# First gates of a two-block kernel: x in four transfers, squares summed pair by pair, rstd spread from its own column; HGRN2 scores of both directions in one call

## The chip, the cores and the metric

The kernel runs on one core of a Trainium2 chip. The metric is the device time of one execution in microseconds; lower is better. The time before is 875.5 us, the median of three runs (874.65 to 876.54).

## The reference

Two transformer-like blocks on 256 latent tokens and 256 context tokens of width 1024, all in 32-bit floats. The change touches the opening of the first block and the core of its HGRN2 mixer.

```python
m_l = (sc_lat @ w_ada + b_ada); m_c = sc_ctx @ w_ada + b_ada   # shift, scale, gate ...
hl = modulate(rmsnorm(lat, norm_g[0]), sh1, sc1)               # x*rstd*g*(1+scale)+shift
hc = modulate(rmsnorm(cx, norm_g[0]), csh1, csc1)
...
q, zf_fwd, zf_bwd, v, g = split(h @ w_in, 5)                   # per direction d:
f = lb[d] + (1 - lb[d]) * sigmoid(zf); logf = log(f); k = 1 - f
...
b = cumsum(logf)                                               # in chunks of 64
qe = q * exp(b - b_ref); ke = k * exp(b_ref - b)
scores = where(tril, qe @ ke.T, 0)
o = scores @ v + (q * exp(b)) @ s_start                        # both directions are added
```

After that come the mixer's readout, a convolutional feed-forward layer, and the second block with retention, windowed attention and a squared-ReLU layer; the change leaves them alone.

## The kernel before

Activations stand feature by token: xT is eight tiles (k = 0 to 7) of 128 features by 512 tokens, the context's 256 and the latents' 256. Every weight tile is split into a high part `hi` (ACT, L155) and a low part `lo` (DVE, L156), every activation likewise into hTh and hTl, and a dense product is three matmuls, hi·hi, hi·lo and lo·hi (`mm3`, L352 to L354). PSUM has two sets of four banks, "x" and "m".

All loads stand in one list `halves` in the order of use. `pump` issues them on SP's queue into eight buffers `raw` of 512 KB, as these come free, and emits the splits up to a limit; `use` takes the next chunk of the list. ACT, DVE and TensorE each work in program order, so the order of the code is the order on the engine.

First gates (L438 to L532). SP's queue brings xT in eight transfers, the identity, and then by turns the ada pieces (`ada1`, 1 MB each in two halves, used unsplit) and the f0 weights (256 KB each). 36 filler matmuls (`WARM`) on ones keep TensorE busy meanwhile. x is squared and added up over k, the array sums over features (L473), `rstd_of` makes a scale and a power on GpSimd (L319), DVE puts the four columns on a diagonal `dg` (L477), and one 512-column matmul with ones spreads it over the partitions (L487). `x_r` multiplies a tile of x by it. `ada_mm(k)` (L403) makes shift and scale of the features of tile k from the ada piece, four column groups at a time; `feat(k)` (L412, L413) turns them into columns A and B; `feat_hi` and `feat_lo` make h = x·r·A + B and its two parts. The loop over k then lays f0's four output tiles (forget gates of head pair 0, both directions): one output tile, the feature chain of k + 1 with its splits, three more, then `ada_mm(k + 2)`; the order is written out in `plan`.

HGRN2 (from L618). Head pairs p = 0 to 3. Per pair and direction `gates` makes scaled keys and queries on ACT and DVE, then `hg_side` gives small steps for TensorE: T_ (transposes of keys kc, copied by ACT to kcT at L627), SC_(hh, d) (scores of one head and direction), S_ (state, L633), O_ (output), OT_ (transpose). The steps of pairs 0 to 2 are queued in `side` and `tick` runs the next one at fixed places of the following pair's dense products; two score steps fall on one place. Those of the last pair stand in `slots` (L867 on), at four places in each of the four g products.

SC_ (L638) fills one PSUM bank: eight matmuls whose output takes 32 partitions (L647, L649), one 128-wide (L652), two 64-wide (L658). DVE then copies the kept entries under the mask (L664), ACT copies the rest (L666, L671), and after the second direction DVE adds both into scm.

## Time and profile before

| | |
|---|---|
| time, median of 3 | 875.5 us |
| the profiled execution: time | 873.8 us |
| its span, first to last instruction | 872.0 us |
| TensorE busy | 856.8 us (98%) |
| VectorE busy | 599.5 us (69%) |
| ScalarE busy | 497.8 us (57%) |
| granted TensorE clock, mean | 0.997 |

The span is shorter than the time by 1.8 us, which lie around it. A TensorE that counts as busy need not be at its peak: matmuls overlap, and at a low granted clock they last longer. So the share says where to look, and the timeline of a stretch says what is won there. All times below are microseconds from the start of the span.

### The profile page before, as it was taken

Reading aid. Unit: us, or ns where it says so; the run is one execution under the profiler, and the core shown is the slowest. Engines: PE = TensorE matmul, PEld = TensorE weight load, DVE = VectorE, ACT = ScalarE, POOL = GpSimd, SP = SyncE. Lnnn points to the kernel's source line nnn. Section 1 sums busy time; section 2 is a strip of 40 time slices with the busy share of each in tenths; the row PEclk is TensorE's granted clock in tenths of the full one; section 3 lists DMA queues with packets and bytes.
Section 4 is the critical chain, followed back from the end, with each engine's and each line's share of the span. In section 5 each row is a group of like instructions: output and inputs, shape, how many; then the busy total and the mean of one; then the engine's idle time right before and its main releaser. Section 6 shows DMA issues by size and latency. Waiting matters only on the chain.

```text
span 872.0 us, 15429 instructions
## 1 busy us (share of the span) xinstructions
PE 856.8 (98%) x6216; PEld 778.4 (89%) x6216; DVE 599.5 (69%) x935; ACT 497.8 (57%) x807; POOL 16.3 (2%) x27
## 2 busy tenths in 40 slices
PE   8999999999999999999999999999999999999997
PEld 7688898989978999999998799999999899999995
DVE  5577969776888688977768646765485687555532
ACT  4587474855856666555555646666553675444421
POOL 0000000000000000000000000000000100000000
PEclk9999999999999999999999999999999999999999
DMA  9893653825437368776753574545696097566401
GB/s 355 277 337 109 184 180 125 287 73 170 144 123 240 122 214 272 265 240 203 259 179 85 157 218 119 147 144 165 196 309 201 6 317 247 184 190 190 148 1 49
DMA packets 116360, 161.99 MB, mean 186 GB/s; under 512 B 13888, under 2 KB 95808, under 8 KB 116288
## 3 DMA queue, kind: packets, MB, share of 16 engines
q1 hardware_dynamic: 113984, 155.80, 55.4%
q10 hardware_dynamic: 2304, 5.20, 1.8%
q8 instruction: 49, 0.80, 0.4%
q14 instruction: 23, 0.19, 0.1%
HBM read 159.93 MB, written 1.05 MB: 185 GB/s over the span
## 4 chain that ended last, share of the span: by engine, by line
PE 89%; DVE 5%; ACT 3%; DMA 1%; issue 1%; POOL 0%; SPq 0%; POOLq 0%; DVEq 0%; ACTq 0%
PE m L352 17%; PE m L353 17%; PE m L354 17%; PE x L352 8%; PE x L353 8%; PE x L354 8%; PE x L691 1%; DVE lo L156 1%; PE m L342 1%; PE x L342 1%; PE m L343 1%; PE m L338 1%; PE x L343 1%; PE x L338 1%; DMA raw<-in_f0w_dram 1%
## 5 line engine op out<-in xcount | busy, mean ns | idle before, releaser
L156 DVE TENSOR_TENSOR lo<-raw,hi 128x1024 fp32r<-128x1024 f32 (+1 forms) x248 | 291.1, 1204 | 128.4 <-ACT hi L155 124.5
L155 ACT ACTIVATE hi<-raw 128x1024 fp32r<-128x1024 f32 (+1 forms) x248 | 249.6, 1039 | 115.9 <-PE x L353 47.7
L352 PE MATMUL m<-hT,hi 128*128 128x256 f32 (+1 forms) x560 | 178.2, 318 | 1.4 <-ACT hT L428 1.4
L353 PE MATMUL m<-hT,hi 128*128 128x256 f32 (+1 forms) x560 | 170.5, 304 | 0.5 <-DVE hT L435 0.5
L354 PE MATMUL m<-hT,lo 128*128 128x256 f32 (+1 forms) x560 | 170.8, 305 | 0.1
L352 PE MATMUL x<-hT,hi 128*128 128x256 f32 x592 | 166.5, 281 | 0.0
L353 PE MATMUL x<-hT,hi 128*128 128x256 f32 x592 | 165.9, 280 | 0.0
L354 PE MATMUL x<-hT,lo 128*128 128x256 f32 x592 | 165.9, 280 | 0.0
L352 PEld LDWEIGHTS m<-hT,hi 128*128 128x128 f32 x560 | 105.6, 189 | 12.2 <-issue 5.1
L354 PEld LDWEIGHTS x<-hT,lo 128*128 128x128 f32 x592 | 113.0, 191 | 0.0
L352 PEld LDWEIGHTS x<-hT,hi 128*128 128x128 f32 x592 | 111.4, 188 | 1.0 <-ACT hi L155 0.2
L353 PEld LDWEIGHTS x<-hT,hi 128*128 128x128 f32 x592 | 111.1, 188 | 1.0 <-issue 0.2
L353 PEld LDWEIGHTS m<-hT,hi 128*128 128x128 f32 x560 | 105.7, 189 | 5.9 <-DVE hT L435 1.1
L354 PEld LDWEIGHTS m<-hT,lo 128*128 128x128 f32 x560 | 105.4, 188 | 5.8 <-DVE lo L156 0.3
L352 PE MATMUL m<-hi,ah 128*128 128x512 f32 x248 | 96.7, 390 | 0.0
L354 PE MATMUL m<-hi,al 128*128 128x512 f32 x248 | 96.6, 390 | 0.0
L353 PE MATMUL m<-lo,ah 128*128 128x512 f32 x248 | 96.6, 389 | 0.0
L354 PEld LDWEIGHTS m<-hi,al 128*128 128x128 f32 x248 | 46.6, 188 | 9.8 <-DVE al L1149 0.2
L353 PEld LDWEIGHTS m<-lo,ah 128*128 128x128 f32 x248 | 46.6, 188 | 8.8
L352 PEld LDWEIGHTS m<-hi,ah 128*128 128x128 f32 x248 | 46.5, 188 | 8.7
L582 DVE SCALAR_TENSOR_TENSOR vr<-raw,cs,vr 128x1024 f32<-128x1024 f32 x28 | 35.9, 1281 | 0.4
L352 PE MATMUL m<-hi,hT 128*128 128x256 f32 x128 | 35.8, 280 | 0.0
(302 smaller groups left out, 1250.7 us busy)
## 6 DMA issues: line engine op xcount, KB each, us to landing
raw<-in_ffn_w_up_dram SPq DMA_DIRECT2D x44, 512.0 KB, 5.6
raw<-in_w_in_dram SPq DMA_DIRECT2D x42, 512.0 KB, 4.1
raw<-in_hg_w_in_dram SPq DMA_DIRECT2D x36, 512.0 KB, 5.0
raw<-in_w_ada_dram SPq DMA_DIRECT2D x32, 512.0 KB, 5.0
raw<-in_w_up_dram SPq DMA_DIRECT2D x32, 512.0 KB, 4.7
raw<-in_w_down_dram SPq DMA_DIRECT2D x32, 512.0 KB, 3.7
raw<-in_ffn_w_down_dram SPq DMA_DIRECT2D x22, 512.0 KB, 4.3
raw<-in_ada_dram SPq DMA_DIRECT2D x16, 512.0 KB, 6.2
```

The lines of the kernel that those rows point to most:

```text
L155: s_.activation(h[:, :w], r[:, :w], AF.Copy)
L156: held.append(lambda r=r, h=h, l=l, w=w: v_.tensor_tensor(l[:, :w], r[:, :w], h[:, :w].bitcast(F32), op=OP.subtract))
L338: t_.matmul(o, hTl[:, k, c], w[k][0], start=False, stop=k == KT - 1)
L342: t_.matmul(o, hTh[:, k, c], w[k][0], start=k == 0, stop=False)
L343: t_.matmul(o, hTh[:, k, c], w[k][1], start=False, stop=False)
L352: t_.matmul(o, wh, xh, start=start, stop=False)
L353: t_.matmul(o, wh, xl, start=False, stop=False)
L354: t_.matmul(o, wl, xh, start=False, stop=stop)
L582: v_.scalar_tensor_tensor(acc, w[kk][0], cs[:, k:k + 1], acc, op0=OP.mult, op1=OP.add)
L691: t_.matmul(z[:, b * 128:(b + 1) * 128], l, r, start=i == 0, stop=i == len(terms) - 1)
```

## The change

- xT comes in four transfers of two tiles each (the host lays it out so that a partition's row of a transfer is 4 KB). The ada pieces leave the list of `halves`: they have eight buffers of their own, four pieces deep (`ADA_BUFS`), loaded by `load_ada`; f0's loads are let out one by one behind them (`lim`), and only after the last ada piece the rest of the list.
- 9 fillers in place of 36. The bank of the sums is cleared by a 512-column matmul with zeros; every pair of squared tiles is added and summed by four 128-column matmuls onto it, with one or two fillers behind.
- r is spread by four matmuls that take a column of r, broadcast, against the identity. `ada_mm(0)` and `feat(0)` go ahead of that, `ada_mm(1)` between it and the first f0 product.
- A and r go into one multiplication (`feat_h`), B into the ACT copy for hTh and into the low part. For k = 0 all eight products with hTh go first, the four with hTl last.
- The mask is stored as bytes. The lower bounds are worked out in the loop; ACT loads the table of Exp there and then that of Sigmoid again.
- `SC_(hh)` does both directions: two 128-wide matmuls, then 24 with an output of 32 partitions in turn over the four column groups, then both directions' copies. The last pair's slots put both score steps behind the state steps, and the output steps one place later.

```diff
+ADA_BUFS = 4
-WARM = 36
+WARM = 9
...
-    C["xT"] = add([([(lambda t, k=k: xT[:, k, :], a["xcT"][k]) for k in range(KT)]
+    C["xT"] = add([([(lambda t, k=k: xT[:, k:k + 2, :], a["xcT"][:, k:k + 2, :]) for k in range(0, KT, 2)]
                     + [(lambda t: ident, a["ident"])], 1, 512)], "own")
...
-    def ada_mm(k, w):
+    def load_ada(k):
+        ar[k] = [p0.tile([128, 4, 256], F32, tag="ar", name="ar", bufs=2 * ADA_BUFS) for _ in range(2)]
+        for j in range(2):
+            nc.sync.dma_start(ar[k][j], a["ada1"][k, :, j])
+
+    def load_f0(n=1):
+        at_["lim"] += n
+        pump(0)
+
+    def ada_mm(k):
         rw = bank("x")
         for kk in range(KT):
             g = slice(kk % 4 * 32, kk % 4 * 32 + 32)
-            t_.matmul(rw[g, :256], c2[:, kk, :], w[kk][0], start=kk < 4, stop=kk >= 4)
-        rs[k] = p0.tile([128, 256], F32, tag="rs", name="rs")
+            t_.matmul(rw[g, :256], c2[:, kk, :], ar[k][kk // 4][:, kk % 4, :], start=kk < 4, stop=kk >= 4)
+        rs[k] = p0.tile([128, 256], F32, tag="rs", name="rs", bufs=2)
+        if k + ADA_BUFS < KT:
+            load_ada(k + ADA_BUFS)
+            load_f0(1 if k + ADA_BUFS < KT - 1 else 1 << 20)
         return lambda: s_.activation(rs[k], rw[:, :256], AF.Copy)
-
-    def x_r(k, r_):
-        v_.tensor_mul(xT[:, k, :], xT[:, k, :], r_)
...
+    def feat_h(k, r_):
         AB = hs[k]
         h = p0.tile([128, 512], F32, tag="h", name="h")
+        half = [(slice(256 * i, 256 * i + 256), AB[:, 3 - i:4 - i], AB[:, 1 - i:2 - i]) for i in range(2)]
+        for i, (c, A, B) in enumerate(half):
+            v_.scalar_tensor_tensor(h[:, c], xT[:, k, c], A, r_[i], op0=OP.mult, op1=OP.mult)
+            if k or not i:
+                s_.activation(hTh[:, k, c], h[:, c], AF.Identity, bias=B)
             else:
+                v_.tensor_scalar(hTh[:, k, c], h[:, c], B, None, op0=OP.add)
+        for c, A, B in half:
+            v_.scalar_tensor_tensor(hTl[:, k, c], h[:, c], B, hTh[:, k, c].bitcast(F32), op0=OP.add, op1=OP.subtract)
...
+    warm_up(WARM)
+    sb = bank("x")
+    t_.matmul(sb, zeros, ones[:, 0:1].to_broadcast([128, 512]), start=True, stop=False)
+    sq = {}
+    for k in range(KT):
+        sq[k] = p0.tile([128, 512], F32, tag="sq", name="sq", bufs=4)
+        if k in (1, 3, 5):
+            v_.tensor_mul(sq[k], xT[:, k, :], xT[:, k, :])
+        else:
+            s_.activation(sq[k], xT[:, k, :], AF.Square)
+        if k % 2:
+            v_.tensor_add(sq[k], sq[k - 1], sq[k])
+            for i in range(4):
+                t_.matmul(sb[:, i * 128:(i + 1) * 128], sq[k][:, i * 128:(i + 1) * 128], ones, start=False,
+                          stop=k == KT - 1 and i == 3)
+            if k < KT - 1:
+                warm_up(1 + k // 5)
+        if k == 5:
+            for j in range(2):
+                v_.tensor_mul(c2[:, :, j], cs[:, 8 * j:8 * j + 8], vecs[:, 8 * j:8 * j + 8])
+            v_.tensor_mul(cs, cs, vecs[:, 0:16])
+    r = rstd_of(sb.rearrange("p (i t) -> p i t", t=128)[:, :, 0], 4, D)
+    pump(chunks[C["f0", 0]][1])
+    ada_mm(0)()
+    warm_up(2)
+    feat(0)
+    rb = [bank("x") for _ in range(2)]
+    for i in range(4):
+        t_.matmul(rb[i // 2][:, i % 2 * 128:i % 2 * 128 + 128], r[:, i:i + 1].to_broadcast([128, 128]), ident,
+                  start=True, stop=True)
+    ev = ada_mm(1)
+    feat_h(0, [x[:, 0:256] for x in rb])
+    ev()
+    R = p0.tile([128, 512], F32, tag="sq", name="R", bufs=4)
+    for i in range(2):
+        s_.activation(R[:, 256 * i:256 * i + 256], rb[i][:, 0:256], AF.Copy)
+    R = [R[:, 0:256], R[:, 256:512]]
...
+    lb, oml, noml = [early.tile([128, 16], F32, name=n) for n in ("lb", "oml", "noml")]
     for k in range(KT):
+        w = use(C["f0", k], ahead=0)
         if k:
+            f0_mm(w, k, (0,))
+        else:
+            wh, wl = w[0]
+            c = [slice(e * 128, e * 128 + 128) for e in range(4)]
+            for e in range(4):
+                t_.matmul(zf[e], wh[:, c[e]], hTh[:, 0, :], start=True, stop=False)
+                t_.matmul(zf[e], wl[:, c[e]], hTh[:, 0, :], start=False, stop=False)
+        if k + 1 < KT:
+            pump(chunks[C["f0", k + 1]][1])
+            feat(k + 1)
+        if k + 2 < KT:
+            ev = ada_mm(k + 2)
+        if k + 1 < KT:
+            feat_h(k + 1, R)
+            if k == KT - 2:
+                pump(chunks[C["q", 0]][1])
+        if k + 2 < KT:
+            ev()
+        if k == 0:
+            nc.scalar.dma_start(hmask, a["hmask"])
+            for e in range(4):
+                t_.matmul(zf[e], wh[:, c[e]], hTl[:, 0, :], start=False, stop=False)
+        else:
+            f0_mm(w, k, (1, 2, 3))
+        if k == 1:
+            v_.tensor_max(lbt[:, 0], vec("lb0"), vec("lb1"))
+            v_.tensor_sub(lbt[:, 1], vec("lb0"), lbt[:, 0])
+            v_.tensor_sub(lbt[:, 2], vec("lb1"), lbt[:, 0])
+            s_.activation(lbt[:, 1:3], lbt[:, 1:3], AF.Exp)
+        if k == 2:
+            v_.tensor_add(lbt[:, 3], lbt[:, 1], lbt[:, 2])
+            v_.reciprocal(lbt[:, 3], lbt[:, 3])
+            v_.tensor_mul(lb, lbt[:, 1], lbt[:, 3])
+            v_.tensor_scalar(oml, lb, -1.0, 1.0, op0=OP.mult, op1=OP.add)
+            v_.tensor_scalar(noml, oml, -1.0, None, op0=OP.mult)
+            s_.activation(warm, warm, AF.Sigmoid)
...
-        def SC_(hh, d):
+        def SC_(hh):
+            zs, groups = [], [[] for _ in range(4)]
+            for d in range(2):
+                e = el[d]
+                z = bank("x")
+                zs.append(z)
+                b1, b2 = e["blk"]
+                t_.matmul(z[:, 256:384], flat(e["K"][:, hh, b1, e["k"], :]), flat(e["Q"][:, hh, b2, e["c"], :]),
+                          start=True, stop=True)
+                zd = z[:, 0:256].rearrange("p (b t) -> p b t", b=2)
+                zo = z[:, 384:512].rearrange("p (b t) -> p b t", b=2)
+                ha, hb = (0, 32) if d == 0 else (32, 0)
+                for b in range(2):
+                    for i in range(2):
+                        g = 2 * d + i
+                        groups[g].append((zo[32 * g:32 * g + 32, b, :], e["K"][:, hh, b, e["sA"], 32 * i:32 * i + 32],
+                                          e["Q"][:, hh, b, e["sB"], :]))
+                    for c in range(2):
+                        o = hh * 256 + b * 128 + 64 * c
+                        ga, gb_ = 2 * c + ha // 32, 2 * c + hb // 32
+                        rb = slice(32 * gb_, 32 * gb_ + 32)
+                        groups[ga].append((zd[32 * ga:32 * ga + 32, b, 64 * c:64 * c + 64],
+                                           e["ke"][:, o + ha:o + ha + 32], e["qe"][:, o:o + 64]))
+                        groups[gb_].append((zd[rb, b, rb], e["ke"][:, o + hb:o + hb + 32],
+                                            e["qe"][:, o + hb:o + hb + 32]))
+            for n in range(max(len(g) for g in groups)):
+                for g in groups:
+                    if n < len(g):
+                        t_.matmul(*g[n], start=True, stop=True)
...
-    slots = [[], [[T0], [T1], [], [SC00]], [[S0], [SC10, S1], [SC01], [SC11]], [[O0], [O1], [], [OT0]]]
+    slots = [[], [[T0], [T1], [], []], [[S0], [S1], [SC0], [SC1]], [[], [O0], [O1], [OT0]]]
...
-    data["xcT"] = np.concatenate([np.asarray(inputs[n])[0].T.reshape(KT, 128, T) for n in ("ctx", "x")], axis=2)
+    xcT = np.concatenate([np.asarray(inputs[n])[0].T.reshape(KT, 128, T) for n in ("ctx", "x")], axis=2)
+    data["xcT"] = xcT.transpose(1, 0, 2)
```

## Rows read from the trace of the kernel before

**Rows 1.** Page, part 1 (busy us, share, count) and part 4 (chain).

```profile
PE 856.8 (98%) x6216; PEld 778.4 (89%) x6216; DVE 599.5 (69%) x935; ACT 497.8 (57%) x807; POOL 16.3 (2%) x27
...
PE 89%; DVE 5%; ACT 3%; DMA 1%; issue 1%; POOL 0%; SPq 0%; POOLq 0%; DVEq 0%; ACTq 0%
```

**Rows 2.** TensorE waits, whole span: line, releaser, total us, times, longest.

```profile
PE x L705 <- DVE on L699: 0.5, 1, 0.5
...
PE x L691 <- ACT xs L671: 0.3, 1, 0.3
```

**Rows 3.** The tile xT, its last transfer: issue, then time from issue to landing.

```profile
L134 SPq DMA_DIRECT2D xT<-in_xcT_dram x1: 328/328/328, 4.8 to 4.8; - x1
...
DMA to landing us min/median/max: 4.8/4.8/4.8
```

**Rows 4.** The tile raw, second half of the third ada piece: issue, then landing.

```profile
L134 SPq DMA_DIRECT2D raw<-in_ada_dram x1: 328/328/328, 9.6 to 9.6; - x1
...
DMA to landing us min/median/max: 9.3/9.3/9.3
```

**Rows 5.** Busy time by stretch, two early ones; last columns clock, DMA share, GB/s.

```profile
4.00:5.00 1.00, 1.00 (x7) 1.00 (x6) 0.84 (x5) 0.36 (x2) 0.00 (x0) 1.00 1.05 298
...
9.00:10.00 1.00, 1.00 (x11) 1.00 (x10) 1.00 (x3) 0.93 (x2) 0.00 (x0) 1.00 1.04 420
```

**Rows 6.** Timeline, first gates: start us, us, engine, line, operation, idle before.

```profile
6.29 3.94 ACT L462 ACTIVATE sq<-xT 128x512 f32<-128x512 f32 x6
...
11.79 1.05 PE L473 MATMUL x<-ones,sq 128*128 128x2 f32 x8
...
13.12 1.02 POOL L319 TENSOR_TENSOR r<-r,mhalf 128x4 f32<-128x4 f32 x1 [12.68 <-DVE r L327]
...
14.92 1.13 PE L487 MATMUL x<-dg,ones 128*128 128x512 f32 x2 [1.08 <-DVE dg L477]
12.77 1.07 PE L403 MATMUL x<-raw,c 128*32 128x256 f32 x16
...
17.64 1.09 ACT L428 ACTIVATE hT<-xT,AB 128x256 fp32r<-128x256 f32 x2 [1.68 <-DVE AB L416]
...
18.78 0.50 PE L352 MATMUL m<-hT,hi 128*128 128x512 f32 x1 [1.40 <-ACT hT L428]
```

**Rows 7.** Timeline of TensorE, f0 products from k = 1 to their end.

```profile
25.30 0.50 PE L352 MATMUL m<-hT,hi 128*128 128x512 f32 x1
...
29.71 0.50 PE L352 MATMUL m<-hT,hi 128*128 128x512 f32 x1
...
54.17 0.28 PE L352 MATMUL m<-hT,hi 128*128 128x256 f32 x1
```

**Rows 8.** Fillers of line 457 in two stretches: count, then min/median/max ns.

```profile
L457 PE MATMUL x<-ones x4: 421/421/421, 4.7 to 5.3; 128*128 128x128 f32 x4
...
L457 PE MATMUL x<-ones x6: 275/275/275, 6.3 to 6.9; 128*128 128x128 f32 x6
```

**Rows 9.** Busy time by stretch around the fall of TensorE's clock.

```profile
20.00:21.00 1.00, 1.00 (x7) 0.90 (x5) 0.05 (x1) 0.00 (x0) 0.00 (x0) 0.50 1.06 422
...
23.00:24.00 1.00, 1.00 (x5) 0.73 (x4) 0.67 (x2) 0.81 (x2) 0.00 (x0) 0.84 0.57 194
```

**Rows 10.** Timeline of TensorE, two score calls in a row, head pair 0.

```profile
88.19 0.24 PE L647 MATMUL x<-qe,ke 128*32 128x64 f32 x1
...
88.54 0.49 PE L652 MATMUL x<-Q,K 128*128 128x128 f32 x2
...
89.33 0.24 PE L647 MATMUL x<-qe,ke 128*32 128x64 f32 x1
...
90.48 0.50 PE L352 MATMUL m<-hT,hi 128*128 128x512 f32 x1
```

**Rows 11.** Timeline, last head pair: what the first state product waits for.

```profile
240.96 1.08 ACT L627 ACTIVATE kcT<-x 128x512 f32<-128x512 f32 x2
...
241.60 1.16 PE L633 MATMUL x<-vt,kcT 128*128 128x128 f32 x8 [1.38 <-ACT kcT L627]
```

More of the change, by code (lines that the diff above doesn't have):

```diff
@@ L119, in pump @@
             go_on = False
-            while at_["l"] < len(halves):
+            while at_["l"] < min(len(halves), at_["lim"]):
                 i = at_["l"]
@@ L214 @@
     ada_seq = []
-    def ada_chunk(k):
-        C["ada", k] = add([([(whole, a["ada1"][k, :, j])], 4, 256) for j in range(2)], "raw")
-    C["xT"] = add([([(lambda t, k=k: xT[:, k, :], a["xcT"][k]) for k in range(KT)]
+    C["xT"] = add([([(lambda t, k=k: xT[:, k:k + 2, :], a["xcT"][:, k:k + 2, :]) for k in range(0, KT, 2)]
                     + [(lambda t: ident, a["ident"])], 1, 512)], "own")
-    ada_chunk(0)
-    ada_chunk(1)
     for k in range(KT):
         C["f0", k] = add([([(whole, a["f0w"][k])], 1, 512)])
-        if k + 2 < KT:
-            ada_chunk(k + 2)
     for p in range(4):
@@ L293 @@
     v_.memset(warm, 0.0)
-    s_.activation(warm, warm, AF.Exp)
+    s_.activation(warm, warm, AF.Sigmoid)
     vecs = const.tile([128, NVEC], F32, name="vecs")
@@ L312 @@
     v_.memset(ones, 1.0)
-    lbt = early.tile([128, 4, 16], F32, name="lbt")
-    v_.tensor_max(lbt[:, 0], vec("lb0"), vec("lb1"))
-    v_.tensor_sub(lbt[:, 1], vec("lb0"), lbt[:, 0])
-    v_.tensor_sub(lbt[:, 2], vec("lb1"), lbt[:, 0])
-    s_.activation(lbt[:, 1:3], lbt[:, 1:3], AF.Exp)
+    zeros = p0.tile([128, 128], F32, name="zeros", bufs=1)
+    v_.memset(zeros, 0.0)
     def rpow(r):
@@ L446 @@
     use(C["xT"], ahead=0)
+    for k in range(ADA_BUFS):
+        load_ada(k)
+        load_f0()
     hmask = early.tile([128, 2, 128], U8, name="hmask")
[L448 to L451 removed]
+    SplitPool(start, "p0split", 3, chunks[C["f0", KT - 1]][1], 512)
     c2 = early.tile([128, KT, 32], F32, name="c2")
     v_.memset(c2, 0.0)
[L455 to L478 removed]
     bp1 = early.tile([128, 8], F32, name="bp1")
@@ L482 @@
     v_.tensor_scalar(bp2, vec("bsc2"), 1.0, None, op0=OP.add)
-    ev = ada_mm(0, w)
-    R = p0.tile([128, 512], F32, name="R", bufs=1)
-    zf = [bank("m") for _ in range(4)]
-    rb = bank("x")
-    t_.matmul(rb, ones, dg.rearrange("p a b -> p (a b)"), start=True, stop=True)
-    w1 = use(C["ada", 1], keep=C["ada", 0], ahead=0)
-    ev()
-    w = use(C["f0", 0], keep=C["ada", 0], ahead=0)
-    x_r(0, rb)
-    feat(0)
-    h = feat_hi(0)
-    s_.activation(R, rb, AF.Copy)
-    feat_lo(0, h)
-    ada_mm(1, w1)()
@@ L497, with warm_up @@
-    at_["rel"] = chunks[C["f0", 0]][0]
-    x_r(1, R)
-    plan = ["0s123a"] + ["0s123a"] * (KT - 4) + ["0s1a23", "s0123", "0123"]
+    wb = bank("m")
+    def warm_up(n):
+        for _ in range(n):
+            t_.matmul(wb[:, 0:128], ones, ones, start=True, stop=True)
+    warm_up(WARM)
[19 more added lines that the diff above has]
+            v_.tensor_mul(cs, cs, vecs[:, 0:16])
@@ L536 @@
+        if k == 2:
[4 more added lines that the diff above has]
+            v_.tensor_scalar(noml, oml, -1.0, None, op0=OP.mult)
+            s_.activation(warm, warm, AF.Sigmoid)
     start.close()
```

147 lines of the change are left out of this document (28 added, 119 removed).

## The prediction

> **What bounds the kernel now.** I read the page's busy shares first, then its chain of waits: TensorE is busy 856.8 of 872.0 us and the chain that ended last lies 89% on it [rows 1]. So the kernel gets shorter only where TensorE gets less to do, or where it waits or runs at half clock. The list of TensorE's waits names few places in the body; the two that the change touches are 0.5 and 0.3 us [rows 2], and a third, 1.38 us, stands in the last head pair [rows 11]. The rest of what can be won lies ahead of the first dense product. So the second reading is the timeline of the first 55 us: the first f0 product starts at 18.78 [rows 6], the second feature tile's (k = 1) at 25.30, and the first product behind f0 at 54.17 [rows 7]. The third reading is what a score call costs TensorE [rows 10].
>
> **The change, part by part.**
>
> *x arrives.* The last of eight x transfers was issued at 4.8 and landed 4.8 later, at 9.6 [rows 3]. While x streamed the queue moved 298 GB/s, when the larger ada pieces followed it moved 420 [rows 5]. The change asks for x in four transfers with rows of 4 KB, as long as those of ada. At some 400 GB/s from about 2.5 us on, 2.1 MB of x and 0.15 MB of vecs are through near 8.0; I take 8.4 for the last landing. Bounds: 8.0 (420 throughout) and 9.6 (no change).
>
> *Squares and sum.* Before, ACT squared until 10.23 (6.29 + 3.94) in six steps of 0.66, then two adds took until the array began at 11.79, 0.78 each with the hand-over; the array took 1.05 and ended at 12.84 [rows 6]. Now the last pair needs two squares on ACT (1.3), one add (0.78) and 1.05 on the array: 8.4 + 3.1 = 11.5. The three earlier pairs are summed while x still comes in. The zero matmul and the fillers are off the path if TensorE has done them by 10.5. The nine fillers run at the low clock: in the first stretch a filler lasts 421 ns, later 275 [rows 8], which I read as 1.2 and 2.4 GHz. Two passes at about 0.21 (spacing at the low clock) times nine is 3.8, the zero matmul, four times as wide, some 1.7 more, so TensorE is busy from 1.1 to 6.6, when the first pair is ready. From there each pair (1.05) and its filler fit into the 1.25 in which a pair of x arrives. Bound: all pairs at half clock, some 1 us later.
>
> *rstd and its spread.* From the array's end at 12.84 to the power on POOL it is 13.12 + 1.02 = 14.14 [rows 6], 1.30, unchanged: r at 12.8. From there to the first f0 product (18.78) 4.64 passed, with the diagonal, the spread, a whole-tile multiply by r, A and B, and two ACT halves of 0.55 in a row [rows 6]. Now four 128-column matmuls spread r itself; nearest row the array's 1.05. But ada_mm(0) (1.07 [rows 6]), two fillers and feat(0) stand ahead of them on TensorE, until about 13.3: spread at 13.3 to 14.4. Now A, B and r are in one DVE step per half, ACT adds the bias to one half and DVE to the other: about 1.2. hT is ready near 15.5.
>
> *The new queue ahead of f0.* On TensorE ada_mm(1) now stands between the spread and the first f0 product; everything behind it waits for its weights. The third ada piece landed at 9.6 + 9.3 = 18.9 [rows 4], as the last of 5.72 MB. f0's second piece now precedes it, 0.26 MB or 0.6 us at 420 GB/s, and x is 1.2 earlier: 18.3. The second piece ends 1.31 MB ahead of that, 3.1 us: 15.2. So ada_mm(1) runs 15.2 to 16.3, f0 starts at 16.3, not at 15.5. Its eight products with hTh take at most 0.28 each, (4.41 - 1.07) / 12 [rows 6, 7]: 18.4. Then feat(1), ada_mm(2) from 18.8 to 19.9 (its weights at 18.3), four products: k = 1 starts at 20.8. It was 25.30, so **4.5 us** come off; what follows, 28.87 us up to 54.17 [rows 7], has the same TensorE work. Included is the end of a stretch at half clock: the granted clock was 0.50 from 20 and back within the slice of 23 [rows 9], after 1.40 us without work ahead of 18.78 [rows 6]; in the new order TensorE has no such gap there.
>
> *Edits with one answer.* The lower-bound arithmetic moves into the loop, and brings two more table loads on ACT (Exp, back to Sigmoid). ACT is busy 57% [rows 1], a load takes 1.28 [rows 6], and its lag lands on tiles that are used a round of 4.41 later; if that cover is gone, it is 1.3 us each. The mask arrives as bytes, so one DVE cast falls; DVE is not on the path there. In k = 6, without an ada step, the feature chain (A and B, then by halves two DVE steps, two ACT steps of 0.55 [rows 6] and two DVE steps, some 2.8 us in all) has only nine products to hide in; I put that at 0 to 0.8 us, about what that place lost before, and take nothing.
>
> *Scores.* A call cost TensorE 89.33 - 88.19 = 1.14, two in a row with the way back 90.48 - 88.19 = 2.29. The sixteen narrow passes take 0.35 of each, 22 ns a pass; the rest goes to one 128-wide and two 64-wide matmuls, each group entered from another shape [rows 10]. The new call does both directions: two 128-wide matmuls at 0.29 each (eight passes, 1.16 [rows 11]), 0.58, and 24 narrow ones, 48 passes. At 22 ns these are 1.05, at the 13 ns between neighbouring starts some 0.65; I take 0.9, and get 1.5: 0.75 saved per pair, bounds 0.6 (all at 22 ns) and 1.0 (all at 13). Head pairs 0 to 2 have six such pairs and TensorE waits nowhere in them: **4.5 us**, bounds 3.6 and 6.0. DVE and ACT have the same instructions.
>
> The Trainium skill (TensorE: Matmul & The Clock Gate, "Wait — 56ns, not 53.3ns?") has a rule against this part: starts of matmuls are never closer than about 25 ns, however few columns, and the change turns two 64-wide matmuls into four 32-wide ones. By it the 48 passes would be 1.2, an estimate from that page, and the six pairs would give about 3.0. The trace's 16 passes in 0.35 [rows 10] lie just under that floor.
>
> *The last head pair.* Its first state product waits 1.38 us for kcT from ACT, until 241.60 [rows 11]. kcT hangs on ACT and DVE work that the change leaves alone, so it comes no earlier. The score call that stood ahead of this wait (1.14) moves behind it: the wait becomes some 2.6 us and nothing is won ahead of it. Behind it stand two joint calls (3.0) where three single ones (3.45) stood: 0.45 won. The 0.3 us for xs [rows 2] goes, as O0 is one slot later; the 0.5 us wait of the last transpose [rows 2] grows to about 0.9, since O1 is one slot later too: together 0. And 2.6 us without work is more than the 1.40 after which the clock fell [rows 6, 9]. I expect it to fall here: some 3.3 us at half clock as at 20, about 1.6 lost. The last head pair: **-1.2**, bounds +0.8 and -2.0.
>
> **Sum.** 4.5 + 4.5 - 1.2 = 7.8 us off the profiled execution: its span 872.0 becomes 864.2, its time 873.8 becomes 866.0. The median of the runs shown is 875.5, 1.7 above that execution; against it the forecast is 875.5 - 7.8 = 867.7.
>
> **The rivals.**
> - *The clock stays up in the last head pair, and the transfers keep up with the array.* For it: 1.38 us of waiting at 241.60 left the clock alone. Then +0.4 there instead of -1.2, f0 up to 1 us earlier, and scores near the upper bound: 875.5 - 11.5 = 864.0. Chance 0.18.
> - *x comes no earlier.* The 298 GB/s may belong to the first microseconds and not to the 2 KB rows. Then all landings move back by 1.2, ada_mm(1) starts at 16.4, and the first part gives about 3 us; with scores at their lower bound, 3.0 + 3.6 - 1.2 = 5.4: 870.1. Chance 0.12.
> - *The low clock lasts through the first gates.* With 9 fillers in place of 36 TensorE may not be granted the full clock at 6 us, nor again before f0 is dense. At half clock from 6 to about 22, the squares, ada and f0 steps there (some 10 us of work) take up to 5 us more, and the first part gives nothing: 875.5 - 3.3 = 872.2. Against it: TensorE is busy without a gap as long as it was before the rise [rows 8]. Chance 0.08.
> - *Slower: the narrow passes do not run side by side.* If a change of array columns between two PSUM banks makes each pass wait for the one before, 48 passes cost 48 x 0.107 (half of the low-clock spacing of a 128-column pass) or 5.1 us, a joint call 5.7 instead of 2.29: 8 pairs lose 27 us, 875.5 + 27 - 4.5 = 898. It decides from (2.29 - 0.58) / 48 = 36 ns per pass for the part, and from about 50 ns for the whole. Against it: 22 ns with the same four column groups in the same turn [rows 10]. Chance 0.04.
>
> **How the numbers follow.** My forecast 867.7 with its own range 865 to 870 has 0.55, the rivals 0.18, 0.12, 0.08 and 0.04; 0.03 is left for a loss of the first part's gain to something unseen, near no change. The range must reach the first two rivals and the edge of the third: 862.5 to 872.3. A measurement of this kernel tells 0.2% (1.75 us) from no change. Faster by more: 0.90; within: 0.05; slower: 0.05.
>
> **What would show it.** x's last landing near 8.4; the power on POOL starting near 11.8; ada_mm(1) waiting for its piece; f0's first product near 16.3 and the end of f0 near 49.7; no slice at clock 0.50 near 20; joint score calls of about 1.5 us; the state product of the last head pair waiting some 2.6 us, with a lower granted clock just behind. Wrong would be: a wait of f0 products on DVE in each round, kcT that comes earlier, or narrow passes at over 36 ns.

## The result, and the profile after

The changed kernel took 862.11 us in the median (861.55 to 862.88, four executions), the kernel before 875.08 beside it: a ratio of 0.9851, 95% interval 0.9834 to 0.9868. The forecast was 867.7 us, with a range from 862.5 to 872.3. The direction was right; the gain came out at 13.0 us where 7.8 were expected, just past the fast end of the range. The profiled execution took 861.95 us with a span of 860.2, so between the two profiled executions 11.8 us went.

The page of the changed kernel, part 1, and from part 4 the chain of waits by engine, beside [rows 1]:

```profile
span 860.2 us, 15548 instructions
PE 845.8 (98%) x6270; PEld 773.6 (90%) x6270; DVE 601.3 (70%) x947; ACT 491.8 (57%) x801; POOL 16.3 (2%) x27
...
PE 90%; DVE 5%; ACT 4%; issue 1%; DMA 1%; POOL 0%; POOLq 0%; DVEq 0%; ACTq 0%
```

TensorE is busy 11.0 us less and the chain still lies on it; the kernel is bound as it was. Of TensorE's waits over the whole span (line, releaser, total us, times, longest), the longest was 1.38 us before [rows 11], and that of the last transposes is as it was [rows 2]:

```profile
PE x L642 <- ACT kcT L636: 2.5, 1, 2.5
...
PE x L726 <- DVE on L720: 0.5, 1, 0.5
```

The timeline of the first gates after, TensorE and POOL (start, us, engine, line, operation, idle before), answers to [rows 6, 7]:

```profile
11.91 1.16 PE L477 MATMUL x<-ones,sq 128*128 128x128 f32 x8
13.36 1.02 POOL L312 TENSOR_TENSOR r<-r,mhalf 128x4 f32<-128x4 f32 x1 [12.91 <-DVE r L320]
...
16.11 1.07 PE L405 MATMUL x<-ar,c 128*32 128x256 f32 x16
17.24 0.47 PE L514 MATMUL m<-hT,hi 128*128 128x512 f32 x1
...
21.63 0.40 PE L345 MATMUL m<-hT,hi 128*128 128x512 f32 x1
...
49.62 0.28 PE L345 MATMUL m<-hT,hi 128*128 128x256 f32 x1
```

The sums on the array end at 13.0, no sooner than before, and the power on POOL starts 0.24 later than before (13.36 against 13.12). But between it and the first f0 product now lie 3.9 us instead of 5.7: f0 starts 1.54 sooner (18.78 to 17.24), k = 1 3.67 sooner (25.30 to 21.63), and the end of f0 comes 4.55 sooner (54.17 to 49.62). Which of the edits in between (the spread of r, the order of the ada steps, the joined multiplication) gives how much of these 1.8 us was not taken apart.

One joint score call in head pair 1, with the dense product ahead of it and the one behind it, answers to [rows 10]:

```profile
134.34 0.39 PE L347 MATMUL m<-hT,lo 128*128 128x512 f32 x1
134.57 0.60 PE L657 MATMUL x<-Q,K 128*128 128x128 f32 x4
135.11 0.25 PE L678 MATMUL x<-Q,K 128*32 128x64 f32 x2
...
135.61 0.29 PE L678 MATMUL x<-qe,ke 128*32 128x32 f32 x9
135.83 0.50 PE L345 MATMUL m<-hT,hi 128*128 128x512 f32 x1
```

From the last dense start ahead to the first dense start behind it is 135.83 - 134.34 = 1.49 us; two single calls took 90.48 - 87.86 = 2.62 on the same measure. The 48 narrow passes take 135.83 - 135.11 = 0.72, 15 ns each. But not all of this belongs to the passes: the last of them starts at 135.69, so that neighbouring starts lie 12 ns apart on average (0.58 / 47), and 0.14 is the way out, from the last narrow start to the first start of the next shape. The sixteen passes of a single call before lie 14 ns apart, from 88.19 to 88.39 (88.34 + 0.27, less the last one's own 0.22), and its way out to the 128-wide product takes 0.15. Two rows of the kernel before that [rows 10] does not show:

```profile
87.86 0.40 PE L354 MATMUL m<-hT,lo 128*128 128x512 f32 x1
...
88.34 0.27 PE L647 MATMUL x<-qe,ke 128*32 128x64 f32 x3
```

A table of the stretches between landmarks of TensorE, in us of the profiled executions, says where the 11.8 us went. S0 is the first state product of a head pair, OT0 the first transpose of the last pair's output:

| stretch | before | after | gained | forecast |
|---|---|---|---|---|
| start to end of f0 | 54.17 | 49.62 | 4.55 | 4.5 |
| end of f0 to S0 of pair 0 | 44.44 | 43.20 | 1.24 | 1.5 |
| S0 of pair 0 to S0 of pair 1 | 52.08 | 49.99 | 2.09 | 1.5 |
| S0 of pair 1 to S0 of pair 2 | 52.07 | 50.00 | 2.07 | 1.5 |
| S0 of pair 2 to S0 of pair 3 | 38.84 | 38.85 | 0.0 | 0 |
| S0 to OT0 of pair 3 | 22.07 | 20.36 | 1.71 | -1.2 |
| the rest | 608.33 | 608.18 | 0.15 | 0 |

### The profile page after: what moved, and what is told of

Read it like the earlier page. It is cut to its first block, busy times and chain, and to the rows that moved or that the text cites. A ratio compares the mean times of both kernels' runs of the same rounds, so it can differ in the third digit from the quotient of the medians.

```text
span 860.2 us, 15548 instructions
## 1 busy us (share of the span) xinstructions
PE 845.8 (98%) x6270; PEld 773.6 (90%) x6270; DVE 601.3 (70%) x947; ACT 491.8 (57%) x801; POOL 16.3 (2%) x27
## 4 chain that ended last, share of the span: by engine, by line
PE 90%; DVE 5%; ACT 4%; issue 1%; DMA 1%; POOL 0%; POOLq 0%; DVEq 0%; ACTq 0%
PE m L345 17%; PE m L346 16%; PE m L347 16%; PE x L345 9%; PE x L346 8%; PE x L347 8%; PE x L712 2%; PE x L405 1%; PE x L335 1%; PE m L335 1%; PE m L336 1%; PE m L331 1%; PE x L336 1%; PE x L331 1%; PE x L642 1%; DVE lo L158 1%
## 5 line engine op out<-in xcount | busy, mean ns | idle before, releaser
L345 PE MATMUL m<-hT,hi 128*128 128x256 f32 (+1 forms) x556 | 175.4, 315 | 0.0
L346 PE MATMUL m<-hT,hi 128*128 128x256 f32 (+1 forms) x556 | 168.8, 304 | 0.0
L347 PE MATMUL m<-hT,lo 128*128 128x256 f32 (+1 forms) x556 | 168.6, 303 | 0.1
L345 PEld LDWEIGHTS m<-hT,hi 128*128 128x128 f32 x556 | 104.5, 188 | 9.9 <-issue 4.6
L346 PEld LDWEIGHTS m<-hT,hi 128*128 128x128 f32 x556 | 104.7, 188 | 5.4 <-DVE hT L433 0.7
```

The lines of the kernel that those rows point to most:

```text
L345: t_.matmul(o, wh, xh, start=start, stop=False)
L346: t_.matmul(o, wh, xl, start=False, stop=False)
L347: t_.matmul(o, wl, xh, start=False, stop=stop)
```

## The experiments

**The two halves by themselves.** sc_only is the kernel before with the joint call and the new slots alone, gates_only the changed kernel with the single calls and the slots of before.

```
sc_only:    SC_(hh, d) -> SC_(hh), both directions' products together
            slots: [[T0],[T1],[],[]], [[S0],[S1],[SC0],[SC1]], [[],[O0],[O1],[OT0]]
gates_only: SC_(hh) -> SC_(hh, d)
            slots: [[T0],[T1],[],[SC00]], [[S0],[SC10,S1],[SC01],[SC11]], [[O0],[O1],[],[OT0]]
```

> The kernel before with the joint score call and the new slots of the last head pair, nothing else. Theory P (the two parts add up, each as the trace after shows it: f0 ends 4.55 us earlier, the rest of 11.8 comes from the scores): about 7.3 us less than the kernel before, six pairs in head pairs 0 to 2 at 1.1 each, the last pair some 1 to 2 us. Theory Q (as forecast: 0.75 per pair, and a fall of the clock in the last pair): about 3.3 us less. Theory R (the score part is worth 4.7 and the first gates bring the rest by loads that come earlier): about 4.7 less.

> The kernel after with the score calls and the slots of before: only the first gates are new. Theory P: 4.5 us less than before, f0's end near 49.6 as in the trace after, and the last head pair's first state product waits about 1.4 us again. Theory Q: 4.5 too. Theory R: 6 to 8 us less, the distance between f0's end and the last head pair being shorter than in before.

sc_only: 868.80 us in the median, ratio 0.9910 (0.9883 to 0.9936), span 865.5. gates_only: 869.18, ratio 0.9922 (0.9905 to 0.9938), span 867.5. Against the span of 872.0 that is 6.5 and 4.5; together 11.0 of the 11.8. In sc_only's profile f0 ended later than in the kernel before, at 55.00; behind the end of f0 it takes 810.5 us, where the kernel before takes 817.8 and the changed kernel 810.6. So the score half is worth 7.3 by itself and 7.2 in the changed kernel. Against the median of the kernel before on the same chip, 876.45, the two medians give 7.65 and 7.27, together 14.9 where the whole change gives 13.0; two of the four executions of sc_only had a mean clock of 0.988 and took 870.3 and 870.5, the other two 0.997, 865.6 and 867.3. So the halves add up in the profiles, and in the medians to within some 2 us; no sign is there that one hides the other. sc_only alone already shows the longer wait in the last pair; in gates_only it is the old one, 1.4. The first line of TensorE's waits in sc_only:

```profile
PE x L633 <- ACT kcT L627: 2.9, 1, 2.9
```

In gates_only the stretch from S0 to S0 is 52.07, as before; in sc_only it is 49.99 and 49.79. So all of the gain in these stretches is the score call's.

**Joining or narrowing?** per_dir keeps the joint call, but issues its products direction by direction; wide64 keeps them together, but gives zo back its 64-wide passes.

```
per_dir:  for d in range(2):
              128-wide products of d
              24 narrow passes of d          # four column groups in turn for 16 passes, two for the last 8
wide64:   groups[g].append((zo[32 * g:32 * g + 32, ...]))      # 8 of these
       -> wide.append((zo[64 * d:64 * d + 64, ...]))           # 4, behind the narrow passes
```

> The changed kernel with its joint score call, but inside it the products issued direction by direction: four 128-wide ones and 24 narrow ones of one direction (in two column groups of the array), then those of the other; copies stay behind both. Theory M: the narrow passes gain because four of them, in four column groups, run side by side; with two at a time a pass takes about 30 ns where it took 15, so 48 x 15 ns = 0.7 us a pair, six pairs 4.3 us: 866.4. Theory N: a narrow pass takes its 15 ns whichever group it follows, and only one more change between wide and narrow per pair is paid, 0.1 to 0.2 us each, six pairs 0.6 to 1.2 us: 862.7 to 863.3.

> The changed kernel with the zo products of a joint score call in four 64-wide passes behind the narrow ones, as they were before, instead of eight 32-wide ones among them. Theory E: a change of tile width on the array costs about as much as the way from a dense product into a wide one, 0.1 to 0.3 us, and there is one more in each of eight calls: 1 to 2 us slower than the changed kernel, 863 to 864. Theory F: the width costs nothing and four passes of 15 ns are saved: within 0.4 us of the changed kernel.

per_dir: 867.54 us, ratio 0.9922 (0.9907 to 0.9937), span 864.8. One call of per_dir in pair 1 on TensorE's timeline (the dense products are those ahead and behind):

```profile
139.19 0.40 PE L347 MATMUL m<-hT,lo 128*128 128x512 f32 x1
139.42 0.39 PE L658 MATMUL x<-Q,K 128*128 128x128 f32 x2
139.74 0.25 PE L679 MATMUL x<-Q,K 128*32 128x64 f32 x2
...
140.05 0.32 PE L679 MATMUL x<-qe,ke 128*32 128x32 f32 x4
140.30 0.49 PE L658 MATMUL x<-Q,K 128*128 128x128 f32 x2
140.72 0.25 PE L679 MATMUL x<-qe,ke 128*32 128x32 f32 x2
...
141.04 0.33 PE L679 MATMUL x<-qe,ke 128*32 128x32 f32 x4
141.30 0.51 PE L345 MATMUL m<-hT,hi 128*128 128x512 f32 x1
```

From dense to dense 2.11 instead of 1.49: 0.62 more per call. The two runs of 24 narrow passes take 0.56 and 0.58 with their ways out, 23 to 24 ns a pass instead of 15. Their last starts stand at 140.15 and 141.15 (the rows of four, less the last one's own 0.22), so from first start to last it is 415 and 435 ns, where the 48 of the joint call take 576 together: 0.27 of the 0.62. Each run then pays a way out of 0.15, one more than in the joint call: another 0.15. The remaining 0.20 are the 128-wide products, 0.32 and 0.42 instead of 0.54 for both.

Contrary to the expectation, the passes of one direction do not go over two column groups alone: its first sixteen go over all four, its last eight over two. The trace shows both. The first sixteen start within 0.20 and 0.21 us, 13 to 14 ns apart, as in the single calls before; the last eight take 0.21 and 0.22, 27 to 28 ns apart. So theories M and N hold a part each: a pass costs about twice as much where only two groups are left (0.27 per call), and every change of shape is paid (0.35). Eight calls at 0.62 are 5.0 of the 5.4 us between the two medians, which were not taken beside each other.

wide64: 864.03 us beside 862.79 for the changed kernel on the same chip, 1.24 slower, though the executions overlap (862.57 to 864.79 and 861.16 to 864.43); span 860.8. The same call of wide64:

```profile
138.60 0.39 PE L347 MATMUL m<-hT,lo 128*128 128x512 f32 x1
...
139.37 0.57 PE L675 MATMUL x<-qe,ke 128*32 128x64 f32 x32
139.86 0.45 PE L677 MATMUL x<-Q,K 128*64 128x64 f32 x8
140.24 0.51 PE L345 MATMUL m<-hT,hi 128*128 128x512 f32 x1
```

1.64 instead of 1.49: 0.15 per call, eight calls 1.2. The eight 64-wide passes take 0.38 (140.24 - 139.86). Of this 0.15 is their way out; their starts, 139.86 to 140.09, lie within 0.23, no more than the sixteen narrow passes that they stand for (48 take 0.58, the 32 that are left 0.35, from 139.37 to 139.72). So the whole 0.15 is one more change of shape, and by the trace theory E holds. Of the 1.13 us that a joint call saves over two single ones, 0.62 is lost again where the two directions' products aren't mixed and 0.15 where zo goes back to 64-wide passes; the rest wasn't taken apart.

**The low stretch near 20 us.** before_fill is the kernel before with six filler products in the gap ahead of f0.

```
 ada_mm(1):  + for _ in range(6): matmul(rw[:, 256:384], ones, ones)
```

> The kernel before with six filler products of ones (into columns of rw that nothing reads) behind ada_mm(1), in the 1.40 us in which TensorE waits ahead of f0's first product. Theory G: the low stretch near 20 us (granted clock 0.5 for 3.41 us) comes from that idle time, and the change won part of its first-gates gain by having none: the low stretch goes, and the time falls by about half of 3.41 us, 1.7 us, to 873.4. Theory H: the low stretch comes from something else (how thin the work before it is, the ramp itself): it stays, and the time stays within 0.4 us of the kernel before (875.1).

873.75 us, ratio 0.9993 (0.9978 to 1.0008): no difference that can be told. Its profiled span is 871.1, against 872.0. TensorE's timeline around the gap, and busy time of 20 to 24 us (clock, DMA share and GB/s last; 0.58 was the clock of this stretch before):

```profile
19.17 0.49 PE L352 MATMUL m<-hT,hi 128*128 128x512 f32 x1 [0.24 <-ACT hT L430]
...
24.08 0.50 PE L352 MATMUL m<-hT,hi 128*128 128x512 f32 x1
...
25.19 0.51 PE L354 MATMUL m<-hT,lo 128*128 128x512 f32 x1 [0.39 <-DVE lo L156]
```

```profile
20.00:24.00 4.00, 4.00 (x31) 2.74 (x31) 1.60 (x5) 2.25 (x4) 0.00 (x0) 1.00 1.01 405
```

The mechanism of theory G is shown: without the gap the clock stays at its upper level, and from f0's first product to k = 1 it is 24.08 - 19.17 = 4.91 us where it was 6.52, 1.61 less. Its price is not: the fillers push f0 back by 0.39, behind k = 1 VectorE's low parts come late, and at the end of f0 only 0.55 us are left (53.62 against 54.17). A stretch at half clock costs little where other engines are nearly as late.

**Four transfers, and the fillers.** x8 is the changed kernel with x in eight transfers, no_fill the one without fillers.

```
x8:      for k in range(0, KT, 2): xT[:, k:k + 2, :]   ->   for k in range(KT): xT[:, k, :]
no_fill: WARM = 9 -> 0;  warm_up(1 + k // 5) -> warm_up(0);  warm_up(2) left out
```

> The changed kernel with x in eight transfers as before instead of four. Theory T: the number of transfers alone brought nothing (in the changed kernel x's last quarter lands at about 10.0 us where the eight landed by 9.6): eight give 861.4 to 862.4, the sums per pair still end at about 13, and if x lands 0.4 us sooner at most 0.4 us is gained. Theory F: four transfers are what lets the sums keep up with x: with eight, the issues delay the later ones, first gates lose 0.5 us or more, 862.8 to 864.

> The changed kernel without any of its filler products on ones ahead of and between the first sums. Theory C: the fillers are what gives the first gates the full clock; without them the sums, both first ada products and part of f0 run at half speed, the low clock lasts to about 20 us, and the time is 2 to 4 us longer: 864 to 866. Theory D: the transfers set the end of the sums anyway, and the work behind them brings the clock up as soon: under 0.5 us, 862.1 to 862.6.

x8: 863.72 us, span 861.0; no_fill: 863.69, span 861.1; ratios 0.9880 (0.9865 to 0.9895) and 0.9881 (0.9866 to 0.9896), where the changed kernel has 0.9851 and, on another chip, 0.9850. First the tile xT in the changed kernel, its last two transfers, and in x8, the last one (issue, then time to landing):

```profile
L136 SPq DMA_DIRECT2D xT<-in_xcT_dram x2: 424/610/796, 1.7 to 2.1; - x2
...
DMA to landing us min/median/max: 6.9/7.4/7.8
```

```profile
L136 SPq DMA_DIRECT2D xT<-in_xcT_dram x1: 328/328/328, 5.1 to 5.1; - x1
...
DMA to landing us min/median/max: 4.4/4.4/4.4
```

x is there at 2.1 + 7.8 = 9.9 with four transfers and at 5.1 + 4.4 = 9.5 with eight; before it was 9.6 [rows 3]. The four transfers bring x no sooner: over all profiles here it is there between 9.4 and 9.9 with four (ten profiles) and between 9.3 and 9.7 with eight (four). In x8 the last pair of squares is summed sooner, but the ada weights, issued later, are late, and f0 starts at 17.42 instead of 17.24 (TensorE's timeline of x8):

```profile
11.13 1.06 PE L477 MATMUL x<-ones,sq 128*128 128x128 f32 x8
...
13.22 0.64 PE L405 MATMUL x<-ar,c 128*32 128x256 f32 x8 [0.47 <-DMA ar<-in_ada_dram]
...
17.42 0.47 PE L514 MATMUL m<-hT,hi 128*128 128x512 f32 x1
```

At the end of f0 it is 0.2 us behind the first profile of the changed kernel (49.80 against 49.62), and 0.6 behind the second (49.22). So what four transfers bring, as far as these profiles show, is free queue time for the weights, a few tenths of a us; the rest of the 0.9 to 1.6 us between the medians is within the scatter of the changed kernel itself (861.16 to 864.43) and stays open. In no_fill, TensorE's timeline shows the half clock where the fillers had been:

```profile
7.47 3.45 PE L477 MATMUL x<-ones,sq 128*128 128x128 f32 x16 [4.14 <-DVE sq L475]
11.13 2.39 PE L477 MATMUL x<-ones,sq 128*128 128x128 f32 x16 [0.21 <-DVE sq L475]
...
17.69 0.47 PE L513 MATMUL m<-hT,hi 128*128 128x512 f32 x1
```

The first sixteen passes of the sums take 3.45 us instead of the 2.3 (twice 1.16) that they take at the full clock. They free the buffers of the squares later (ScalarE waits 0.56 for one), the last pair is through at 13.45 instead of 13.00, and f0 starts 0.45 later. Theory C falls in its mechanism (the passes lie 0.21 apart until 10.4 and 0.11 from then on; the clock does not stay low to 20), theory D is right in kind and 0.45 at that place. The time, 863.69, lies between the two; the profile also has a fall of the clock in the last pair, which cost 0.95 there (S0 to OT0 21.31 instead of 20.36), and the rest stays open.

**The last head pair.** state_late moves S0 and S1 two steps back; fill_wait puts fillers into the wait ahead of S0; last_old gives the last pair alone its single calls and old slots; pool_gates is state_late with the gate products qe, ke and q2 of this pair on GpSimd.

```
state_late: [[S0],[S1],[SC0],[SC1]], [[],[O0],...]  ->  [[],[],[S0,S1],[SC0]], [[SC1],[O0],...]
fill_wait:  S_(0) of pair 3:  + for _ in range(10): matmul(z[:, 256:384], ones, ones)
last_old:   pair 3 only: SC_(hh) -> SC_(hh, d), slots as in gates_only
pool_gates: state_late, and for p == 3: vector.tensor_mul(qe, ..), (ke, ..), q2 -> gpsimd
```

> The kernel after with the last head pair's steps moved: both state steps to the third place of g2, score step 1 to the first place of g3. The wait of 2.5 us for kcT has two places (2.8 us) of dense product ahead of it that stood behind it before. Theory P (the wait is pure loss, nothing behind it is late): 2 to 2.5 us less than the kernel after. Theory S (the chain behind it, state to output to the last transpose, takes the wait's place): within 0.7 us of the kernel after, with the wait of the last transposes up from 0.5 to 2 us or more.

> The kernel after with ten filler matmuls on ones ahead of the last head pair's first state product, in the 2.5 us in which TensorE waits for kcT. They need about 2.2 us at the full clock. Theory F (the wait makes the clock fall in some executions; the trace after shows one without a fall, mean clock 0.999, other executions had 0.997): all executions at 0.999 and the median 0.5 to 1 us under the kernel after. Theory G (the wait never costs the clock; 0.997 comes from another place): same time as the kernel after within 0.3 us, clocks spread from 0.997 to 0.999 as before.

> The changed kernel with the last head pair's scores in the four single calls and the slots of before; the other three pairs keep the joint call. Theory P (the forecast): behind S0 the joint call gains only 0.45 us there, so this is at most 0.5 us slower than the changed kernel, and if the joint call brings a low stretch with it, up to 1 us faster: 861.1 to 862.6. Theory Q (the trace of the changed kernel): behind S0 the joint calls gain 1.7 us and cost nothing ahead of it, since the wait for kcT comes from the work before: 1.7 us slower, 863.8, with the wait for kcT still at 2.5.

> The changed kernel with S0 and S1 two steps later in the last head pair (as in state_late, 864.5, where TensorE waited 4.2 us for the low part of the weights, which stood behind the gates on VectorE), and with three of the gate products of this pair (qe, ke and q2, some 4 us of VectorE in all) on GpSimd. Theory D: VectorE's work ahead of that low part is what the last pair waits for: the wait falls to under 1.5 us, no low stretch follows, and the time is 859.5 to 862. Theory R: GpSimd takes so much longer for them (128x512 products; its 128x8 power took 1.0 us) that the scores wait for it instead: 864 or more.

> The changed kernel itself, beside the three others on one chip, for their comparison and for how far its executions differ. Theory V: in the last head pair the wait of 2.5 us for kcT stands at the edge, so that in some executions a low stretch follows it and in some not (mean granted clock 0.997 and 0.999 so far): times in two groups some 0.8 us apart, 861.5 to 863, and stretches of dense products differ by 0.4 us between executions of the same code. Theory W: the executions agree within 0.3 us and with the first ones, 862.1.

What bounds this place is read from the chain of waits of the changed kernel between 205 and 235 us, in order of time (start, us, what): for some 27 us it does not touch TensorE.

```profile
205.01 0.48 ACT q L765
...
231.76 0.14 DVE q L865
231.93 1.23 DVE lo L158
```

In the kernel before the chain runs over the same steps:

```profile
214.96 0.49 ACT q L745
...
241.71 0.13 DVE q L845
```

It is 26.75 us long in both (231.76 - 205.01, 241.71 - 214.96), and from S0 of pair 2 to S0 of pair 3 every kernel with S0 in its old slot, before or changed, took 38.84 to 38.85 us (twelve profiles). So kcT comes no sooner whatever TensorE does, and a score call ahead of S0 costs nothing there. What kcT itself waits for is its turn on ScalarE, which works without a gap from 223.56 until it comes to the copy; in this stretch lie the last of the gates' exponentials, two splits of weights and a table load of 1.28:

```profile
231.02 1.07 ACT L636 ACTIVATE kcT<-x 128x512 f32<-128x512 f32 x2
```

state_late (864.53, 2.4 above the changed kernel's first median) shows what is late next: the wait for kcT is gone, and one of 4.2 us has come for the low part of the g weights, which stands behind the gates on VectorE (the first line of TensorE's waits):

```profile
PE m L347 <- DVE lo L158: 4.2, 1, 4.2
```

pool_gates shortens that wait to 2.7, and the time is 862.92 (ratio 0.9851, where state_late has 0.9865), level with the changed kernel (862.79 beside it). Theory D is right that VectorE's work ahead of that low part is what the place waits for, but not in the size: the wait did not fall under 1.5, the clock fell behind it (at 231.0), and the time stayed above 862. Theory R's 864 did not come either. GpSimd is a slow helper. GpSimd's and VectorE's timelines:

```profile
230.15 2.01 POOL L848 TENSOR_TENSOR qe<-qe,q 128x512 f32<-128x512 f32 x1
```

```profile
228.26 0.68 DVE L851 TENSOR_TENSOR K<-K,k 128x512 f32<-128x512 f32 x1
...
230.94 1.77 DVE L912 TENSOR_TENSOR oTs<-oTs,sg 128x512 f32<-128x512 f32 x1
```

A product that takes VectorE 0.68 takes GpSimd 2.01, and while GpSimd works, a product of the same size takes VectorE 1.77. The Trainium skill (SBUF — State Buffer, "SBUF: two separate sides") says that the two engines share a port pair, and that whichever starts first, GpSimd or a VectorE instruction with two inputs from SBUF, blocks the other for the whole instruction. The row at 230.94 agrees: it ends at 232.71, 0.55 behind GpSimd's product (232.16). The row at 228.26 kept its 0.68 although a step of GpSimd was under way (q, 227.91 to 229.34), so not every overlap costs VectorE time.

last_old: 863.42 us, 0.6 above the changed kernel beside it, too little to be told from it by the times, with a span of 861.4. Its wait for kcT is 1.38 again, and from S0 to OT0 it takes 22.39 where the changed kernel's first profile has 20.36. Theory P said 0.45 at most behind S0; it falls. Theory Q's 1.7 behind S0 is there (S0 to the last transpose is 23.23, in the changed kernel 21.51), but its wait of 2.5 is not: the call that moves back ahead of S0 fills 1.1 of it.

**How much the clock matters there.** after_again is the changed kernel again: 862.79 us in the median, four executions from 861.16 to 864.43. In its profile the clock fell behind the wait, which is 2.87 us here, and in the first profile, with 2.52, it did not. Busy time from 232 to 235 of after_again and then of the first profile (clock third from the right):

```profile
232.00:235.00 3.00, 3.00 (x19) 3.00 (x18) 3.00 (x4) 2.56 (x5) 0.00 (x0) 0.61 0.51 150
```

```profile
232.00:235.00 3.00, 2.85 (x25) 2.65 (x24) 3.00 (x5) 2.75 (x5) 0.00 (x0) 1.00 0.17 33
```

S0 to OT0 is 21.39 with the fall and 20.36 without: the fall costs 1.03. Of seven profiles with a wait for kcT of 2.5 to 2.9 us, it fell in three (after_again, no_fill, per_dir) and not in four (the first of the changed kernel, x8, wide64, sc_only). In six of them the wait is the same 2.87, so its length does not decide. The eight executions of the changed kernel go with it: three with a mean clock of 0.999 took 861.2 to 862.0, four with 0.997 took 862.1 to 863.5, one with 0.994 took 864.4. Theory V holds in kind; its two groups are not sharp. fill_wait takes most of the wait away: it is 0.6 there, the mean clock 0.998 to 0.999 in all four executions, its time 861.38 to 862.15, median 861.68, ratio 0.9833 (0.9818 to 0.9848). That is the best version here, 0.4 to 1.1 us below the changed kernel's two medians, too little to be told from it.

## Why the prediction was wrong in size

Two terms of the sum failed. The last head pair was put at -1.2 and brought +1.7, above all because a fall of the clock worth 1.6 was put into the sum in full. The scores were put at 4.5 and brought 5.4, because the narrow passes were priced too dear. The first gates' 4.5 came out right by luck: their steps did not.

- **First gates, 4.5: right in sum, by luck.** Forecast: x at 8.4, sums' end 11.5, f0 from 16.3, its k = 1 at 20.8, its end at 49.7. Measured: 9.9, 13.0, 17.24, 21.63 and 49.62. The step "x arrives" failed: the 298 GB/s that it put down to 2 KB rows stayed with 4 KB rows (297 from 4 to 5 us in the changed kernel). x8, with 2 KB rows again, has x no later, and that is rival B. The step on the new queue failed the other way: ada_mm(1) did not wait for its weights (no idle time ahead of 16.11), since the chain ahead of it was late by then. k = 1 is 0.8 late and the end of f0 is on time, because the rounds behind it became shorter as well (27.99 us from k = 1 to the end of f0, 28.87 before), on which the forecast counted for nothing. The end of the low stretch near 20 was called rightly (granted clock 1.00 from 20 to 24); before_fill shows both that the gap made it and that by itself it is worth 0.55 at the end of f0.
- **Scores, 4.5: mis-sized, 5.4 measured.** A pair of calls saves 2.62 - 1.49 = 1.13, not 0.75. The forecast's own terms, 0.58 and 0.9 against 2.29, give 0.81, which it rounded down. The term that failed is the 48 narrow passes: put at 0.9, they took 0.72. The 22 ns a pass that bounded them came from 0.35 for sixteen, of which 0.15 is the way out, paid once and not by each pass; 48 passes at the 13 ns between neighbouring starts with one way out would have been 0.77. The rest is small: the 128-wide part took 0.54 and not 0.58, and the way in, which was left out on both sides, fell from 0.33 (88.19 - 87.86) to 0.23 (134.57 - 134.34). Six times 1.13 would be 6.8; pair 0 gave back 1.0. There the joint call needs both directions' K at once, and in after_again's timeline it waits 0.76 for the second in its middle, which the single calls did not: a wait that the change added and the forecast ("TensorE waits nowhere in them") passed over. From the call's first product to its first narrow pass it takes 1.57 there (83.14 to 84.71) instead of 0.54, which is the 1.0. The first profile loses as much in all: its call stands 0.35 longer, and the dense products ahead of it, spaced some ns wider, took the rest; the second K comes 35.1 us behind the end of f0 in both. The remaining 0.4 are dense products spaced some ns wider in the first profile in pairs 1 and 2; in after_again, x8 and no_fill, with the same code there, they are not (49.79 from S0 to S0), so it is no effect of the change.

```profile
83.14 0.38 PE L657 MATMUL x<-Q,K 128*128 128x128 f32 x2
84.29 0.49 PE L657 MATMUL x<-Q,K 128*128 128x128 f32 x2 [0.76 <-DVE K L856]
```

- **The rule on narrow matmuls.** The Trainium skill's floor of about 25 ns between starts (TensorE: Matmul & The Clock Gate, "Wait — 56ns, not 53.3ns?") would make the 48 passes 1.2 us, an estimate. They took 0.72, and their starts lie 12 ns apart on average. Where only two column groups are left, in per_dir, starts lie 27 to 28 ns apart, above that floor; with four it does not hold, and the measurement decides. The forecast's row of sixteen passes in 0.35, "just under that floor", spoke against it more clearly than it was read: without the way out it is 14 ns a pass.
- **The last head pair, -1.2: wrong in sign, +1.7.** That nothing is won ahead of S0, and that the wait grows to 2.6 (2.52), was right, and last_old and the chain show why. Three things behind it were not. The three places with calls behind S0 took 2.27, 1.35 and 2.78 from dense start to dense start, with the second state step in the first and another matmul in the last, and now take 0.93, 1.37 and 2.95: 1.15 won instead of 0.45, since a single call there costs 1.35 with its way in and out, not 1.15, and a joint one 1.37, not 1.5. The waits for xs (0.3 [rows 2]) and for the last transpose were said to cancel; the first went, and O0 takes 1.82 instead of 2.41 from dense to dense, 0.6 less, while the second stayed at 0.5 and did not grow to 0.9. And the fall of the clock, put into the sum in full at 1.6, is not in the first profile at all; as far as the mean clocks tell, it came in five of the eight executions, and it cost 1.0 where a profile shows it.
- The sum of these differences: 0.9 on the scores, 0.7 on the calls and 0.6 on the waits of the last pair, 1.6 for the clock, 0.2 elsewhere; 4.0, the distance between 7.8 and 11.8. The last 1.2 us up to 13.0 lie in the executions: the one profiled of before was 1.3 below its median. Its mean clock was 0.997; beside the later runs 22 of 27 executions of the kernel before had 0.996 or less, and of the eight of the changed kernel one. So part of these 1.2 us may be time at the lower clock that the change did away with; no profile here shows where.
- **The rivals.** A (clock stays up, scores near their upper bound) names what happened in the scores and the last pair, but for its transfers; B is right on x and wrong on what follows from it; C is refuted by the changed kernel's own clock and by no_fill; D by 15 ns per pass, way out included.

## What to carry to other kernels

Measure a small operation between the same two neighbours in both versions, from the last dense start ahead to the first dense start behind, since the way in and out of an odd tile shape is much of its price. Take that way (0.15 us here) out of the mean of a short run before multiplying it by the number of passes: it is paid per change of shape, not per pass. Where the chain of waits leaves the engine that bounds the kernel, work taken off that engine ahead of the place turns into a wait and only work behind it counts: find such places by a stretch that keeps its length in every version (38.84 to 38.85 us here). Merging two calls also merges their inputs: ask which call comes first and whether the later input is there.

## What the hardware did that was not expected

- Starts of narrow passes that go over four column groups of the array lay 12 to 14 ns apart, over two groups 27 to 28 (per_dir); each way out of them to a wider shape took 0.14 to 0.15 us.
- The same 2.5 to 2.9 us without work for TensorE brought half clock in three profiles and none in four; before, 1.40 us did it near 20 us, and filling that gap prevented it, while 1.38 us ahead of the last pair's S0 did not.
- x as four transfers of 512 KB, all issued by 2.1 us, was there no sooner (9.4 to 9.9, ten profiles) than as eight of 256 KB, the last issued at 4.8 to 5.2 (9.3 to 9.7, four profiles).
- GpSimd took 1.3 to 2.2 us for a 128x512 product that takes VectorE 0.68, and VectorE took up to 1.77 for one meanwhile (pool_gates).
